# A third operand pair for the context tiles, low parts also on POOL, x's squares and scaling ahead of its columns, and eight context tiles in front of x's first columns

## The chip, the cores and the metric

The kernel runs on one core of a Trainium2 chip. The core has a matrix engine (TensorE, PE in the profile, with its weight loads as PEld), a vector engine (VectorE, DVE), an activation engine (ScalarE, ACT), a general engine (GpSimd, POOL) and a queue that issues most of the transfers (SyncE, SP). The metric is the device time of one execution in microseconds. Before the change it is 2383.04 us, the median of three runs from 2377.91 to 2387.13.

## The reference

One layer over 2048 latent tokens of width 1024, behind a prefix of 256 context tokens. All data is fp32.

```python
hc = modulate(rmsnorm(ctx, norm_mix), csh1, csc1)          # context, 256 tokens
logf_f, k_f, logf_b, k_b, vc = hgrn2_gates(hc @ w_in[:, :1536], ...)   # 4 heads x (forward gate, backward gate, value)
hf_c = advance_state(0, k_f, vc, cumsum(logf_f))           # final context state of each head, forward
hb_c = advance_state(0, flip(k_b), flip(vc), cumsum(flip(logf_b)))

h = modulate(rmsnorm(x, norm_mix), sh1, sc1)               # latent, 2048 tokens
p = h @ w_in                                               # 3584 columns: gates, value, query, output gate, two SGU halves
o = concat(bidirectional gated scan starting from hf_c, hb_c;  chunked spatial gating unit)
x = x + g1 * (o @ w_out)
x = x + g2 * conv_ffn(modulate(rmsnorm(x, norm_ffn), sh2, sc2), w_up, conv_w, conv_b, w_down)
return rmsnorm(x, norm_final)
```

`sh1, sc1` and `csh1, csc1` come from a small matrix product of `silu(c)` and `silu(c_ctx)` with `w_ada`. The change touches only the first part: the normalised context, its twelve projections (four heads, three each), the first 1024 latent tokens, and the order of their projections.

## The kernel before, in words

**Products of high and low parts.** Each fp32 operand is split into a rounded high part and a low part, the difference. ACT makes the high part with a copy, another engine subtracts it from the original (`split`, L137 and L138). A product then takes three matmuls: high x high, high x low, low x high. The tiles are called `whi`, `wlo` (weights), `chl` and `cll` (context), `xh` and `xl` (latent).

**Tiles and banks.** A tile of weights is 1024 x 128, so one tile has 1024 elements in each of 128 partitions, and 8 blocks along the contraction. A context tile multiplies it with the 256 context tokens: 24 matmuls of 256 columns. A bank of x multiplies it with 512 latent tokens: 24 matmuls of 512 columns, and two banks use one weight tile. `run_banks` (L523 and following) runs over a list of banks. At the start of each bank it splits the weights of the current and the next key where that hasn't been done, and loads raw weights one further ahead while context tiles are among the next three. Raw weights have three buffers, split weights have two pairs (`whi0`, `wlo0`, `whi1`, `wlo1`); `w_free` lists the free ones. A pair becomes free when the last bank of its key has been issued; the split that takes it then waits for the products that read it. A finished bank stays in one of three PSUM banks `pj` until ACT has read it (the sink).

**The order of the first banks.** `seq` gives it by letters: c a context tile (twelve of them: forward gate, backward gate, value of head 0, then head 1 and so on), g the output gate of latent head 0 (two banks: the first half of the 1024 tokens, then the second), v its value, q its query, s and t the SGU banks of heads 0 and 1 (Gelu on ACT, the others use sigmoids or copies). Then the gate banks of head 0 follow (`back`).

**The prologue** is written out by hand (`manual_schedule`): the order of the instructions on each engine is the order of the lines. It loads `w_ada` in four groups of 2 MB (`load_ada`, halves of 1 MB), squares and scales the context rows, transposes them, makes the modulation vectors (`ada_products`, `ada_rows`, `ada_columns`), and from them the context columns by `ctx_mod`, for k = 0 to 3 when the scale's first half is there and for k = 4 to 7 (`LAST`) after the second half. `keep_busy(n)` issues n products of the identity that nothing reads. In between it opens the first two context tiles with their blocks 0 to 3. Outside of the prologue the order on an engine is chosen when the program is built, by priorities and estimated durations; instructions passed through `pin` keep their order.

**x's columns.** Four row blocks of x (`xg`, 512 tokens) are squared on ACT with their sum (`x_square`), turned into a scale on POOL (`rstd`), scaled on DVE (`x_scale`), transposed on TensorE and modulated in `x_first`: `x_mod` has DVE compute the shifted value from PSUM, ACT the rounded high part, and DVE the low part. `x_start` does that for the first 512 tokens (`x0a`), then for the second (`x0b`, tiles `xk`). The first g bank waits for `x0a`, the second for `x0b`. `x_second` prepares the other 1024 tokens and stores them to DRAM; it must be through before the gate banks of head 0.

**Pumps.** Side work is written as generators in two queues (`bg_q`, `hg_q`). `slot()` is called after a bank and, in banks of 512 columns, between blocks; it advances a queue by one step when the estimated TensorE time `T.t` has passed the step's due time (the number it yielded). `need` forces all steps up to a mark.

Of the kernel before, what the change touches and what calls it, by code (L numbers as in the profile page):

```python
# [18 lines left out]
P = 128  # L19
# [69 lines left out]
def tile_trunk(ctx, tc, x, c, cx, c_ctx, w_ada, b_ada, norm_mix, norm_ffn, w_in, hg_norm, sgu_g, sgu_b,  # L89
# [105 lines left out]
    with es1:  # L195
# [16 lines left out]
        def keep_busy(n):  # L212

            t = bank("pj")
            for i in range(n):
                T.matmul(t[:, :P], ident, ident, start=True, stop=True)
# [3 lines left out]

        w_raw, w_free = {}, [0, 1]

        def load_raw(key):
            raw = raw_tile().rearrange("p (k c) -> p k c", c=P)
            ld(raw, w_in[:, key[0]:key[0] + P].rearrange("(k p) c -> p k c", p=P))
            w_raw[key] = raw

        def split_w(key, eng=V):
            if key not in w_raw:
                load_raw(key)  # L230
            raw, at = w_raw.pop(key), w_free.pop(0)
            hi = p1.tile([P, NK, P], F32R, tag=f"whi{at}", name="whi", align_bytes=AL)
            lo = p1.tile([P, NK, P], F32R, tag=f"wlo{at}", name="wlo", align_bytes=AL)
            split(hi, lo, raw, eng)
            return hi, lo, at
# [99 lines left out]
        with tc.manual_schedule():  # L335
# [9 lines left out]
            load_ada(1)  # L345
            load_ada(3, 0)
            load_raw((HW, CTX))
            load_ada(3, 1)
            S.activation(sg, cc, AF.Sigmoid)
# [34 lines left out]
            ctx_products(0, range(4))  # L384
            keep_busy(16)
            ada_products(3, 0, 4)
            nxt[HW, CTX] = split_w((HW, CTX))
            ada_products(3, 4, 8)
            ada_rows(3)
            opened[HW, CTX] = bank("pj")  # L390
            ctx_products(HW, range(2))
            ada_columns(3)
            ctx_products(HW, range(2, 4))
            ss0 = x_sums()
            for k in LAST:
                ctx_mod(k)
            x_square(xg[:1], ss0, keep=lambda i: i)
        xl = p1.tile([P, NK, TH], F32R, tag="xl", name="xl", align_bytes=AL)
        xh = p1.tile([P, NK, TH], F32R, tag="xh", name="xh", align_bytes=AL)

        def x_first(g0, xs):
            for k in range(NK):
                pt = bank("mi")
                for i in range(4):
                    pin(T.transpose(pt[:, i * P:(i + 1) * P], xs[i][:, k * P:(k + 1) * P], ident))
                sl = slice(g0 * P, g0 * P + 512)
                x_mod(pt, 0, k, xh[:, k, sl], xl[:, k, sl], 512, V)
                if k % 2:
                    yield 1.6
# [3 lines left out]
        def x_start():  # L413
            xk = [pk.tile([P, 2, D], F32, tag="K", name="xk", bufs=2, align_bytes=AL) for i in range(2)]
            xs = [xk[i // 2][:, i % 2, :] for i in range(4)]
            ss, ss2 = ss0, x_sums()
            for q in range(2):
                x_square(xg[2 * q + 1:2 * q + 3], ss, 2 * q + 1)
                for i in range(2 * q, 2 * q + 2):
                    pin(ld(xs[i], x_rows[4 + i]))  # L420
                if q:
                    x_scale(xg, ss)
                yield 2.0 + 3.0 * q
            for i, w in enumerate(x_first(0, xg)):
# [98 lines left out]
        def run_banks(banks, peek=None):  # L523
# [3 lines left out]
            for i, (col, n0, n, sink, pre) in enumerate(banks):  # L527
                if pre is not None:
                    pre()
                up = list(dict.fromkeys(keys[i:] + tail))  # L530
                for key in up[:2]:
                    if key not in nxt:
                        nxt[key] = split_w(key)
                if len(up) > 2 and up[2] not in w_raw and up[2] not in nxt and any(k[1] == CTX for k in up[:3]):
                    load_raw(up[2])
                hi, lo, at = nxt[keys[i]]
# [13 lines left out]
                if keys[i] not in keys[i + 1:]:  # L550
                    w_free.append(nxt.pop(keys[i])[2])

# [529 lines left out]
        seq = []  # L1082
        for item in "c c c c c c g c g v c v q c q s c s s c s t c t t t".split():
            seq.append(parts[item].pop(0))
# [795 lines left out]
```

## Time and profile before

| | |
|---|---|
| median of three runs | 2383.04 us (2377.91 to 2387.13) |
| the profiled execution | 2386.56 us, span 2384.8 us |
| TensorE busy | 2343.6 us, 98% |
| VectorE busy | 1597.3 us, 67% |
| ScalarE busy | 1041.6 us, 44% |
| GpSimd busy | 873.5 us, 37% |
| granted clock, mean | 0.996 |

The profile is one execution. Each row of a timeline is the start, the duration and the engine of an instruction or of several merged ones, its line in the kernel, the operation, the tiles out<-in, the shape, and in square brackets how long the engine was idle before it and what ended that. Rows of groups give the count, the busy time and the mean duration in ns. Rows of stretches give the busy time of every engine between two times. Matmuls overlap, so the distance between two starts says more than the duration of one.

### The profile page before, as it was taken

Reading aid. Unit: us, or ns where it says so; the run is one execution under the profiler, and the core shown is the slowest. Engines: PE = TensorE matmul, PEld = TensorE weight load, DVE = VectorE, ACT = ScalarE, POOL = GpSimd, SP = SyncE. Lnnn points to the kernel's source line nnn. Section 1 sums busy time; section 2 is a strip of 40 time slices with the busy share of each in tenths; the row PEclk is TensorE's granted clock in tenths of the full one; section 3 lists DMA queues with packets and bytes.
Section 4 is the critical chain, followed back from the end, with each engine's and each line's share of the span. In section 5 each row is a group of like instructions: output and inputs, shape, how many; then the busy total and the mean of one; then the engine's idle time right before and its main releaser. Section 6 shows DMA issues by size and latency. Waiting matters only on the chain.

```text
span 2384.8 us, 37077 instructions
## 1 busy us (share of the span) xinstructions
PE 2343.6 (98%) x14155; PEld 1933.1 (81%) x14155; DVE 1597.3 (67%) x2168; ACT 1041.6 (44%) x1814; POOL 873.5 (37%) x787
## 2 busy tenths in 40 slices
PE   7999999999999999999999999999999999999998
PEld 6887878778888877887788888888888888888887
DVE  3757795465687775665786666559777764776876
ACT  3654444443444543544544444344444443332343
POOL 0022111110122231003787877878788860000002
PEclk8999999999999999999999999999999999999999
DMA  8365444373445426679532222742322249734745
GB/s 310 115 198 182 160 152 163 135 239 107 155 160 186 151 90 221 210 229 298 181 99 93 75 91 85 277 152 84 104 79 94 86 137 386 258 127 159 222 150 203
DMA packets 304088, 393.59 MB, mean 165 GB/s; under 512 B 32646, under 2 KB 215710, under 8 KB 300838
## 3 DMA queue, kind: packets, MB, share of 16 engines
q1 hardware_dynamic: 300620, 390.46, 48.9%
q8 instruction: 111, 1.82, 0.3%
q10 hardware_dynamic: 3289, 0.76, 0.2%
q14 instruction: 68, 0.55, 0.1%
HBM read 283.60 MB, written 107.55 MB: 164 GB/s over the span
## 4 chain that ended last, share of the span: by engine, by line
PE 50%; issue 2%; POOL 1%; DMA 1%; DVE 0%; ACT 0%; SPq 0%; POOLq 0%; ACTq 0%; DVEq 0%
PE ux L70 19%; PE dn L70 16%; PE uz L70 14%; DMA raw<-in_w_up_dram 1%; POOL rr L1740 0%; DMA yf<-yd 0%; POOL Al L138 0%; DMA xn<-cv 0%; POOL ra L1739 0%; POOL ra L1737 0%; DVE fl L138 0%; PE ux L74 0%; ACT jk L1728 0%; ACT yst L137 0%; POOL raw L1254 0%
## 5 line engine op out<-in xcount | busy, mean ns | idle before, releaser
L1445 DVE SCALAR_TENSOR_TENSOR dn<-gp,taps,dn 128x1024 f32<-128x1024 f32 x352 | 448.2, 1285 | 97.1 <-ACT dn L1442 92.7
L70 PE MATMUL dn<-thl,mhl 128*128 128x512 f32 x1680 | 381.0, 389 | 0.0
L70 PEld LDWEIGHTS dn<-thl,mhl 128*128 128x128 f32 x1680 | 315.3, 188 | 65.6 <-issue 0.2
L138 POOL TENSOR_TENSOR Al<-raw,Ah 128x512 fp32r<-128x512 f32 x264 | 341.6, 1309 | 70.7 <-ACT Ah L137 40.3
L70 PE MATMUL pj<-xh,whi 128*128 128x512 f32 x896 | 366.8, 410 | 0.0
L70 PE MATMUL pj<-xl,whi 128*128 128x512 f32 x896 | 352.3, 393 | 0.0
L70 PE MATMUL pj<-xh,wlo 128*128 128x512 f32 x896 | 351.3, 392 | 0.0
L137 ACT CAST Ah<-raw 128x512 fp32r<-128x512 f32 x264 | 163.1, 620 | 242.5 <-PE ux L70 125.0
L70 PE MATMUL ux<-xah,Ah 128*128 128x512 f32 x528 | 205.9, 390 | 0.4 <-ACT keep L1509 0.3
L70 PEld LDWEIGHTS pj<-xh,whi 128*128 128x128 f32 x896 | 168.6, 188 | 39.0 <-issue 7.2
L70 PEld LDWEIGHTS pj<-xh,wlo 128*128 128x128 f32 x896 | 168.7, 188 | 35.9
L70 PEld LDWEIGHTS pj<-xl,whi 128*128 128x128 f32 x896 | 169.2, 189 | 29.8 <-DVE xl L257 0.6
L70 PE MATMUL dn<-wo,o 128*128 128x512 f32 x768 | 182.3, 394 | 0.0
L70 PE MATMUL uz<-yf,Ah 128*128 128x512 f32 x704 | 174.0, 389 | 0.0
L70 PEld LDWEIGHTS dn<-wo,o 128*128 128x128 f32 x768 | 142.1, 188 | 29.0
L589 POOL TENSOR_TENSOR K<-K,tot 128x512 f32<-128x512 f32 x40 | 61.2, 1530 | 259.4 <-DVE K L589 152.6
L70 PE MATMUL ux<-yf,Ah 128*128 128x512 f32 x528 | 155.4, 389 | 0.0
L70 PEld LDWEIGHTS uz<-yf,Ah 128*128 128x128 f32 x704 | 132.1, 188 | 27.4
L70 PE MATMUL ux<-xah,Al 128*128 128x512 f32 x528 | 141.8, 390 | 1.6 <-POOL Al L138 1.6
L70 PE MATMUL ux<-xal,Ah 128*128 128x512 f32 x352 | 137.1, 389 | 0.0
L1737 POOL TENSOR_SCALAR ra<-ss 128x1 f32<-128x1 f32 x8 | 3.2, 397 | 359.5 <-ACT jk L1728 359.5
L138 DVE TENSOR_TENSOR wlo<-raw,whi 128x1024 fp32r<-128x1024 f32 x68 | 83.6, 1230 | 74.8 <-ACT whi L137 63.7
(333 smaller groups left out, 4243.4 us busy)
## 6 DMA issues: line engine op xcount, KB each, us to landing
raw<-in_w_up_dram SPq DMA_DIRECT2D x88, 512.0 KB
mr<-m SPq DMA_DIRECT2D x85, 512.0 KB
raw<-in_w_in_dram SPq DMA_DIRECT2D x68, 512.0 KB
sT<-wd SPq DMA_DIRECT2D x88, 256.0 KB
raw<-in_w_ada_dram SPq DMA_DIRECT2D x32, 512.0 KB
yf<-yd SPq DMA_DIRECT2D x14, 1024.0 KB
m<-cv SPq DMA_DIRECT2D x22, 544.0 KB
raw<-in_w_down_dram SPq DMA_DIRECT2D x22, 512.0 KB
```

The lines of the kernel that those rows point to most:

```text
L70: return self.engine.matmul(out, lhsT, rhs, **kw)
L137: keep(S.copy(hi, raw))
L138: (eng or G).tensor_sub(lo, raw, hi.bitcast(F32))
L589: e.tensor_mul(view(K2, row * W + o, src), view(K, o, src), view(tot, t0, [[4, n], [ts, 2], [0, B]]))
L1445: V.scalar_tensor_tensor(out=cr, in0=gt[:, t // 3:t // 3 + RH, t % 3:t % 3 + GW], scalar=taps[:, t * NF + f:t * NF + f + 1], in1=cr, op0=A ...
L1737: G.tensor_scalar(out=a, in0=ss, scalar1=plus, scalar2=None, op0=ALU.add)
```

## The change

The third pair of operand tiles lies in the buffers of two tiles that are needed only later (`qs` and `T1`), and only context tiles may use it. `pair` chooses a pair: the third if it is free, or else the one that has been free longest. `run_banks` splits one key further ahead where the next free pair is the third, loads raw weights up to two keys ahead, and has every other split of a context tile subtract on GpSimd in place of VectorE. The third pair is given up when fewer than six context tiles are left. In the prologue the last half of `w_ada` is loaded ahead of the second context tile's weights; the filler products go from 16 to 20; the second context tile is no longer opened there and is split after the modulation vectors; the third context tile is split there, with its low part on GpSimd; and all four row blocks of x are squared there. `x_start` then starts with a pause and the scaling. For odd k the low part of x's columns in `x_first` is subtracted on GpSimd. In `seq` eight context tiles, not six, come before the first g bank, and all twelve come before the first q bank.

```diff
--- before.py
+++ after.py
@@ -218,19 +218,25 @@
         def raw_tile():
             return p1.tile([P, D], F32, tag="raw", name="raw", bufs=3)
 
-        w_raw, w_free = {}, [0, 1]
+        w_raw, w_free, w_more, n_split = {}, [2, 0, 1], [2], []
 
         def load_raw(key):
             raw = raw_tile().rearrange("p (k c) -> p k c", c=P)
             ld(raw, w_in[:, key[0]:key[0] + P].rearrange("(k p) c -> p k c", p=P))
             w_raw[key] = raw
 
+        def pair(key):
+            return max([a for a in w_free if a < 2 or key[1] == CTX], key=lambda a: (a == 2, -w_free.index(a)), default=None)
+
         def split_w(key, eng=V):
             if key not in w_raw:
                 load_raw(key)
-            raw, at = w_raw.pop(key), w_free.pop(0)
-            hi = p1.tile([P, NK, P], F32R, tag=f"whi{at}", name="whi", align_bytes=AL)
-            lo = p1.tile([P, NK, P], F32R, tag=f"wlo{at}", name="wlo", align_bytes=AL)
+            raw, at = w_raw.pop(key), pair(key)
+            w_free.remove(at)
+            pool, tags = (ph, ("qs", "T1")) if at == 2 else (p1, (f"whi{at}", f"wlo{at}"))
+            kw = {} if at == 2 else {"align_bytes": AL}
+            hi = pool.tile([P, NK, P], F32R, tag=tags[0], name="whi", **kw)
+            lo = pool.tile([P, NK, P], F32R, tag=tags[1], name="wlo", **kw)
             split(hi, lo, raw, eng)
             return hi, lo, at
 
@@ -343,9 +349,8 @@
             load_ada(0)
             load_raw((0, CTX))
             load_ada(1)
-            load_ada(3, 0)
+            load_ada(3)
             load_raw((HW, CTX))
-            load_ada(3, 1)
             S.activation(sg, cc, AF.Sigmoid)
             V.tensor_mul(cs2.rearrange("p k w -> p w k"), cc, sg)
             V.tensor_copy(cs4[:, :, :2], cs2)
@@ -382,19 +387,16 @@
             ada_columns(1)
             opened[0, CTX] = bank("pj")
             ctx_products(0, range(4))
-            keep_busy(16)
-            ada_products(3, 0, 4)
+            keep_busy(20)
+            ada_products(3, 0, 8)
+            ada_rows(3)
+            ada_columns(3)
             nxt[HW, CTX] = split_w((HW, CTX))
-            ada_products(3, 4, 8)
-            ada_rows(3)
-            opened[HW, CTX] = bank("pj")
-            ctx_products(HW, range(2))
-            ada_columns(3)
-            ctx_products(HW, range(2, 4))
-            ss0 = x_sums()
             for k in LAST:
                 ctx_mod(k)
-            x_square(xg[:1], ss0, keep=lambda i: i)
+            nxt[2 * HW, CTX] = split_w((2 * HW, CTX), G)
+            ss0 = x_sums()
+            x_square(xg, ss0, keep=lambda i: i)
         xl = p1.tile([P, NK, TH], F32R, tag="xl", name="xl", align_bytes=AL)
         xh = p1.tile([P, NK, TH], F32R, tag="xh", name="xh", align_bytes=AL)
 
@@ -404,7 +406,7 @@
                 for i in range(4):
                     pin(T.transpose(pt[:, i * P:(i + 1) * P], xs[i][:, k * P:(k + 1) * P], ident))
                 sl = slice(g0 * P, g0 * P + 512)
-                x_mod(pt, 0, k, xh[:, k, sl], xl[:, k, sl], 512, V)
+                x_mod(pt, 0, k, xh[:, k, sl], xl[:, k, sl], 512, G if k % 2 else V)
                 if k % 2:
                     yield 1.6
 
@@ -413,14 +415,14 @@
         def x_start():
             xk = [pk.tile([P, 2, D], F32, tag="K", name="xk", bufs=2, align_bytes=AL) for i in range(2)]
             xs = [xk[i // 2][:, i % 2, :] for i in range(4)]
-            ss, ss2 = ss0, x_sums()
-            for q in range(2):
-                x_square(xg[2 * q + 1:2 * q + 3], ss, 2 * q + 1)
-                for i in range(2 * q, 2 * q + 2):
-                    pin(ld(xs[i], x_rows[4 + i]))
-                if q:
-                    x_scale(xg, ss)
-                yield 2.0 + 3.0 * q
+            ss2 = x_sums()
+            yield 5.0
+            x_scale(xg, ss0)
+            for i in range(2):
+                pin(ld(xs[i], x_rows[4 + i]))
+            yield 5.0
+            for i in range(2, 4):
+                pin(ld(xs[i], x_rows[4 + i]))
             for i, w in enumerate(x_first(0, xg)):
                 if i in (1, 2):
                     x_square(xs[2 * i - 2:2 * i], ss2, 2 * i - 2)
@@ -528,11 +530,13 @@
                 if pre is not None:
                     pre()
                 up = list(dict.fromkeys(keys[i:] + tail))
-                for key in up[:2]:
-                    if key not in nxt:
-                        nxt[key] = split_w(key)
-                if len(up) > 2 and up[2] not in w_raw and up[2] not in nxt and any(k[1] == CTX for k in up[:3]):
-                    load_raw(up[2])
+                for j, key in enumerate(up[:3]):
+                    if key not in nxt and pair(key) in ((0, 1, 2) if j < 2 else (2,)):
+                        nxt[key] = split_w(key, G if key[1] == CTX and len(n_split) % 2 else V)
+                        n_split.append(key)
+                for key in up[2:3 + len(w_more)]:
+                    if key not in w_raw and key not in nxt and any(k[1] == CTX for k in up[:3]):
+                        load_raw(key)
                 hi, lo, at = nxt[keys[i]]
                 hiT, loT = (chl, cll) if n == CTX else (xh, xl)
                 pj = opened.pop(keys[i], None)
@@ -548,7 +552,13 @@
                 sink()(n0, n, pj[:, :n])
                 slot()
                 if keys[i] not in keys[i + 1:]:
-                    w_free.append(nxt.pop(keys[i])[2])
+                    at = nxt.pop(keys[i])[2]
+                    if at == 2 and len([k for k in keys[i:] if k[1] == CTX]) < 6:
+                        w_more.clear()
+                    elif at == 2:
+                        w_free.insert(0, at)
+                    else:
+                        w_free.append(at)
 
         def tile_banks(col, sink, W=TH, pre=None):
             return [(col, n0, min(512, W), sink, pre if n0 == 0 else None) for n0 in range(0, W, 512)]
@@ -1080,7 +1090,7 @@
               (front[1][0], 512, 512, front[1][3], lambda: need(bg_q, "x0b"))]
         parts = {"c": ctx_banks, "g": xa, "v": front[2:4], "q": front[4:6], "s": sgu_banks(0, 0), "t": sgu_banks(0, 1)}
         seq = []
-        for item in "c c c c c c g c g v c v q c q s c s s c s t c t t t".split():
+        for item in "c c c c c c c c g c c g v c v c q q s s s s t t t t".split():
             seq.append(parts[item].pop(0))
         assert not any(parts.values())
         seq += with_post(back, ctx_last)
```

## The prediction

> **What bounds the kernel now.** I read the page first, then busy time by stretch, then TensorE's timeline in the stretches where it is idle or slow.
>
> ```profile
> PE 2343.6 (98%) x14155; PEld 1933.1 (81%) x14155; DVE 1597.3 (67%) x2168; ACT 1041.6 (44%) x1814; POOL 873.5 (37%) x787
> PE 50%; issue 2%; POOL 1%; DMA 1%; DVE 0%; ACT 0%; SPq 0%; POOLq 0%; ACTq 0%; DVEq 0%
> ```
> ```profile
> 41.00:97.10 56.10, 49.63 (x298) 42.90 (x297) 45.98 (x73) 33.87 (x60) 2.42 (x4) 0.91 0.46 139
> 44.00:47.00 3.00, 3.00 (x16) 3.00 (x16) 1.28 (x3) 1.05 (x3) 0.00 (x0) 0.50 0.96 363
> 47.00:51.50 4.50, 1.74 (x9) 1.08 (x9) 1.50 (x2) 3.57 (x6) 1.22 (x2) 0.88 0.37 112
> 51.50:57.30 5.80, 5.80 (x28) 5.80 (x29) 4.01 (x6) 0.92 (x3) 0.00 (x0) 0.50 0.66 186
> 64.00:68.00 4.00, 3.96 (x27) 2.98 (x26) 4.00 (x8) 3.70 (x7) 0.00 (x0) 1.00 0.47 140
> 76.00:81.00 5.00, 2.87 (x21) 2.10 (x20) 5.00 (x8) 2.82 (x5) 0.00 (x0) 1.00 0.15 42
> 130.00:200.00 70.00, 68.88 (x382) 57.42 (x382) 47.55 (x110) 38.50 (x64) 24.08 (x31) 1.00 0.57 183
> ```
> Columns of the second fence: stretch, length, then busy time of PE, PEld, DVE, ACT, POOL, the granted clock, DMA share, GB/s. TensorE sets the end: 98% busy, and first in the chain. So the change is worth what it takes out of TensorE's losses, and those lie in one place. I number the context tiles c0 to c11.
>
> ```profile
> 41.92 0.39 PE L70 MATMUL pj<-ch,whi 128*128 128x256 f32 x1 [0.78 <-ACT whi L137]
> 43.18 0.38 PE L70 MATMUL pj<-ch,wlo 128*128 128x256 f32 x1 [0.76 <-DVE wlo L138]
> 50.02 0.38 PE L70 MATMUL pj<-ch,whi 128*128 128x256 f32 x1 [1.54 <-ACT whi L137]
> 58.02 0.28 PE L70 MATMUL pj<-ch,wlo 128*128 128x256 f32 x1
> 58.14 0.28 PE L70 MATMUL pj<-ch,whi 128*128 128x256 f32 x1
> 63.32 0.60 PE L74 MATMUL mi<-ident,cS 128*128 128x128 f32 x4
> 63.76 1.04 PE L74 MATMUL mi<-ident,xg 128*128 128x128 f32 x8
> 80.61 0.66 PE L74 MATMUL mi<-ident,xk 128*128 128x128 f32 x4 [1.47 <-ACT xh L256]
> 104.98 0.39 PE L70 MATMUL pj<-xh,wlo 128*128 128x512 f32 x1
> 105.21 0.39 PE L70 MATMUL pj<-xh,whi 128*128 128x512 f32 x1
> ```
> Matmuls overlap, so I count by their starts: a context product takes 0.12 us (58.02 to 58.14), an x product 0.23, a transpose 0.11; at clock 0.50 a context product takes 0.21 (28 instructions in the 5.80 us from 51.5). From 41.0 to 97.1 us TensorE did five context tiles (c2 to c6, 24 products each) and three x banks (24 each); the other 106 of its 298 instructions are transposes and small products. That is 120 x 0.119 + 72 x 0.228 + 106 x 0.11 = 42.4 us, in 56.1. **13.7 us are lost there**, in three ways: waits for the next tile's split operand (c2 at 41.9 and 43.2, c3 at 50.0); about nine microseconds at half clock right behind those waits, some 4 us of loss; and the wait for x's second group of columns around 76 to 81, while DVE is busy all the time. From 97 to 200 almost nothing is lost (68.88 of 70 busy at the end).
>
> **The change part by part.** The prologue first.
>
> ```profile
> 29.33 3.73 PE L70 MATMUL pj<-ident 128*128 128x128 f32 x32
> 32.99 1.96 PE L70 MATMUL pj<-wa,cs 128*32 128x128 f32 x64
> 30.07 1.05 ACT L137 CAST whi<-raw 128x1024 fp32r<-128x1024 f32 x1 [5.06 <-DMA raw<-in_w_in_dram]
> 36.01 0.17 DVE L304 TENSOR_TENSOR a<-sc,bc 128x8 f32<-128x8 f32 x1 [0.70 <-PE sc L74]
> 36.47 0.56 ACT L320 ACTIVATE ch<-mi,s,a 128x256 fp32r<-128x256 f32 x1 [5.35 <-DVE a L306]
> 39.92 0.43 DVE L322 TENSOR_TENSOR cl<-xfl,ch 128x256 fp32r<-128x256 f32 x1
> ```
> Four more fillers (8 of 32 instructions that took 3.73) push the last modulation products 0.9 us back, so the scale is ready near 37.1 rather than 36.4. The filler covers a load, the 1 MB half of the modulation weights, which is now issued ahead of c1's weights; c1's weights land later by that megabyte, 2.6 us at the 390 GB/s of the page, so near 32.7, still ahead of their new place behind the scale. There c1's low part (1.22) stands on DVE in front of the last four context columns: they end near 41.5, not 40.35 (the 0.7 later scale and the 1.22, less 0.7 in which DVE waits for ACT there today). Twelve of c1's products leave the gap before the scale and go after it, where they fill the wait for those columns. c0 and c1 are done at 42.0 against 41.1 (41.92 less the idle 0.78): **0.9 lost**.
>
> ```profile
> L243 ACT ACTIVATE xjk<-xg 128x1024 bf16<-128x1024 f32 x3 | 3.2, 1060 | 0.0
> L137 ACT CAST whi<-raw 128x1024 fp32r<-128x1024 f32 x7 | 7.3, 1047 | 5.2 <-PE pj L70 4.4 <-ACT xh L256 0.8
> L138 DVE TENSOR_TENSOR wlo<-raw,whi 128x1024 fp32r<-128x1024 f32 x7 | 8.5, 1219 | 6.2 <-ACT whi L137 6.0
> L613 DVE TENSOR_TENSOR_SCAN cS<-cS,ones_r 128x256 f32<-128x256 f32 x3 | 2.0, 682 | 0.0
> L254 DVE TENSOR_SCALAR xfl<-mi,a,s 128x512 f32<-128x512 f32 x10 | 7.6, 798 | 0.0
> L257 DVE TENSOR_TENSOR xl<-xfl,xh 128x512 fp32r<-128x512 f32 x10 | 6.5, 680 | 0.2 <-ACT xh L256 0.2
> L249 DVE TENSOR_SCALAR xg<-xg,rs 128x1024 f32<-128x1024 f32 x4 | 2.7, 748 | 0.0
> ```
> ```profile
> 41.78 0.38 ACT L558 ACTIVATE cS<-pj 128x256 f32<-128x256 f32 x1
> 73.88 1.36 DVE L257 TENSOR_TENSOR xl<-xfl,xh 128x512 fp32r<-128x512 f32 x2 [0.17 <-ACT xh L256]
> ```
> ```profile
> L138 POOL TENSOR_TENSOR Al<-raw,Ah 128x512 fp32r<-128x512 f32 x264 | 341.6, 1309 | 70.7 <-ACT Ah L137 40.3
> ```
> ```profile
> 139.00 0.75 POOL L257 TENSOR_TENSOR sp<-xfl,sp 128x256 fp32r<-128x256 f32 x1 [0.23 <-ACT sp L256]
> 141.82 1.32 POOL L257 TENSOR_TENSOR sp<-xfl,sp 128x256 fp32r<-128x256 f32 x1 [2.08 <-ACT sp L256]
> ```
> **Low parts on POOL.** No row has a 1024-element one. From below: 2 x 1.309 = 2.6 us. From above: the same 256-element subtraction took 0.75 and 1.32, so 2.6 x 1.76 = 4.6. I take 3.3, nearer the lower end, because DVE subtracts only part of the time. The Trainium skill, "GPSIMD Engine Reference", section 3.1, gives about 2.6 cycles per element at 1.2 GHz, an estimate of 2.2 us; by it c2 below would lose 0.5. Its section 1 says that POOL's SBUF interfaces are shared with VectorE; the 1.32 row agrees.
>
> **c2.** The third pair lets it be split ahead of c0's end. Its high part follows the last context column on ACT (39.5 to 40.5), its low part on POOL ends near 43.8. TensorE is free at 42.0 and has two products that don't need it: **1.6 lost** (0.9 to 2.9).
>
> **The four squares** stand on ACT behind that, 4 x 1.06 to 1.26, to about 45; what queues behind them are the four sigmoids of c0 and c1 (0.38 each, some 1.1 with their overlap; they free PSUM banks) and c3's high part. That is then ready at 47.0 and its low part (V) at 48.2, while c2 ends at 46.4: **1.6 lost** (0 to 2.5). c3 starts 3 us sooner than now.
>
> **The clock.** The trace shows half clock for 3.4 us from 43.7 and 6.8 from 50.6, behind stretches with waits. The waits of c2 and c3 are shorter, not gone; I count two such spells: **3.0 lost** (0 to 4.5). The Trainium skill, "TensorE: Matmul & The Clock Gate", Part 1, says that a window of about 3.4 us decides, and that it runs freely; the spells agree with its length, and by that rule the number of spells in the changed kernel also depends on where a wait falls. By the rule that only an idle window throttles, waits of 1.6 would cost nothing and the sum would be 3 better; the row of 44 to 47, behind two waits of 0.8 us, speaks against it.
>
> **c4 to c7.** From here a split uses a pair that was freed a tile earlier (third pair), so the copy needn't wait for the products before; the alternate low parts on POOL (1.05 + 3.3, against 2.9 us of a tile) start two tiles ahead. I allow **1.0** (0 to 3).
>
> **x's columns.** Squares done early, x_scale runs at about 48 to 51. DVE then has 8 x 0.80 + 4 x 0.68 for x's columns (the other four low parts go to POOL), two context low parts (2.4) and the scans of two context heads with their products (four of 0.68, four shorter ones I put at 0.42): 4.4. Done near 68. TensorE by then has 11.5 for c4 to c7, 3.5 for transposes and 3.4 for context states behind c3's end at 52.5 (48.2, its last 22 products, and one half-clock spell): near 71. The columns, finished today at 75.2 (row 73.88) with DVE full, no longer come last, with 3 us to spare. c8 and c9 after the first x bank cover the second group, today's wait at 76 to 81. But c9 is between the two banks of one key: one pair is held, the third retired after c7, so its split starts when c8 ends: 1.05 + 3.3, against transposes and the second x bank. I take **1.5** (0 to 4.4) for both.
>
> **Behind it.** The context tiles leave the SGU banks, so sigmoids and Gelus alternate less:
> ```profile
> L693 ACT ACT_TABLE_LOAD x2 | 2.6, 1283 | 0.0
> ```
> Each load is 1.28 us of ACT; TensorE's idle there is 1.1 us in 70, so I take 0.4 won (0 to 1.1). The second half of x, which begins behind x's second group, moves with it:
> ```profile
> 88.22 0.82 SPq L442 DMA_DIRECT2D xk<-in_x_dram x2
> 201.39 0.36 SPq L460 DMA_DIRECT2D xh_d<-sp  x1
> ```
> It takes 113 us today and frees the buffers of the first gate tiles. If it ended 8 us later, their sigmoids would wait; three PSUM banks (16 us of products) cover that, so nothing.
>
> **Sum.** Losses 0.9 + 1.6 + 1.6 + 3.0 + 1.0 + 1.5 = 9.6 in place of 13.7, and 0.4 won later: 4.5 us. The profiled execution took 2386.56 (span 2384.8 and 1.8 around it), so 2382.1; the median of the runs, 2383.04, lies 3.5 below it, so **2378.5**.
>
> **Rivals.** (A) Nearly all loss goes: no half clock, c3 and c9 covered by other products. Left are 0.9 and c2's 0.9: 12 us won, 2371. For it: DVE and ACT had room from 41 to 60. Against: the four squares in a block. (B) Slower: POOL's low parts gate TensorE. At 4.6 us, c2 loses 1.3 more, c4 1.7, c6 0.6, c9 4.2, and two more half-clock spells 3.0: 10.8, so 6.3 slower than before, 2389. It decides from about 4 us per low part, if a further clock spell comes with it. For it: the 1.32 row. Against: c4 to c8 can start early. (C) The wait only moves: x's columns, with POOL's subtractions at 2 us and context low parts ahead of them on DVE, end at 72 or later, TensorE waits 4 again before the first x bank: 2382.5. For it: DVE was full from 64 to 68 and from 76 to 81. Against: it sheds six low parts and eight subtractions, 12.8 us.
>
> **Chances.** Forecast 0.42, A 0.25, C 0.20, B 0.13. The runs of before spread over 9 us, so 0.5% (12 us) is about what can be told from no change. Faster by that needs under 2371: over half of A and a little of the forecast, 0.17. Slower needs over 2395: part of B, 0.05. The range takes in A and most of B: 2366 to 2390; the forecast alone is 2374 to 2383.
>
> **What would show it.** Right: c2 starts near 42 and c3 near 47; POOL's 1024-element rows at 3 to 3.6; squares in a block from 40.5 to 45; one or two half-clock spells before 60; first x bank ahead of 72, no gap at the second group; c9 waiting for its low part. Wrong: any low part above 4, a half-clock spell behind 60, new gaps from 97 to 200, or c3 later than 50.

## The result and the profile after

The changed kernel takes **2395.77 us** (median of 6 runs, 2393.42 to 2398.19) against 2383.35 of the kernel before beside it (6 runs, 2377.91 to 2387.13): 12.4 us more, ratio 1.0053, 95% interval 1.0038 to 1.0067. The forecast was 2378.5. The profiled execution took 2394.83 us with a span of 2393.0, so 8.3 more than the one of before, 2386.56. That one lay 3.2 above its median, so the two profiles show less than the medians do. The 4 us between the two differences are seen in no profile.

First a line of the page of the kernel after, then its windows, then one window of before for comparison. The line numbers of after are 6 to 13 higher than those of before. The columns of the windows are stretch, length, busy time and count of PE, PEld, DVE, ACT and POOL, the granted clock, DMA share and GB/s.

```profile
PE 2343.8 (98%) x14163; PEld 1936.2 (81%) x14163; DVE 1598.6 (67%) x2155; ACT 1035.8 (43%) x1810; POOL 895.4 (37%) x800
```
```profile
41.00:60.00 19.00, 15.04 (x117) 14.01 (x117) 14.44 (x15) 13.17 (x26) 8.92 (x5) 1.00 0.60 193
60.00:82.00 22.00, 18.69 (x128) 17.40 (x128) 20.14 (x33) 15.41 (x29) 5.25 (x4) 0.92 0.56 170
82.00:130.00 48.00, 43.92 (x267) 38.21 (x268) 26.89 (x36) 21.84 (x40) 12.89 (x11) 0.96 0.33 99
130.00:200.00 70.00, 69.62 (x351) 57.47 (x349) 38.80 (x98) 30.00 (x51) 22.32 (x28) 1.00 0.59 191
200.00:230.00 30.00, 26.87 (x126) 22.04 (x126) 18.39 (x28) 14.00 (x25) 5.54 (x8) 0.89 0.58 178
```
```profile
41.00:60.00 19.00, 14.70 (x80) 13.70 (x79) 11.22 (x18) 9.55 (x19) 1.22 (x2) 0.73 0.69 209
```

The stretch the change was made for did improve: 117 matmuls from 41 to 60 in place of 80, and the clock 1.00 in place of 0.73. Some 33 of the 117 are products of c0 and c1 that the kernel before had finished by 42; what was won shows at c5, whose first product starts at 59.37 in place of 60.38, although the prologue was late. **POOL's busy time there went from 1.2 to 8.9 us, and DVE, which was to be relieved, went up**: 14.4 us for 15 instructions, against 11.2 for 18. What was won is lost again behind 60.

The same instruction later in both kernels gives the sum (TensorE's timeline, before and then after):

```profile
708.41 1.47 PE L74 MATMUL mi<-ident,K 128*128 128x128 f32 x12
```
```profile
717.34 1.47 PE L74 MATMUL mi<-ident,K 128*128 128x128 f32 x12
```

It is 8.9 us later, so the whole difference of the two profiles, 8.2 us of span, arises in the front. The table counts TensorE's loss there as the prediction did: the distance from one matmul's start to the next, less 0.228, 0.119 or 0.11 us for its size. It is good to about 1 us. The kernels below the first two are the experiments of the next section. Each row is one execution: that of E5 is the fastest of its 12 (2378.98, their median 2385.38), so its row shows less than E5 usually loses.

| us lost | 40 to 60 | 60 to 80 | 80 to 100 | 100 to 180 | 180 to 220 |
|---|---|---|---|---|---|
| before | 9.9 | 3.3 | 0.4 | 1.7 | 0.4 |
| after | 7.9 | 2.0 | 8.1 | 0.2 | 6.5 |
| E1 weights' low parts on DVE | 4.2 | 5.1 | 2.8 | 0.5 | 4.3 |
| E2 all low parts on DVE | 4.2 | 1.7 | 2.1 | 1.1 | 6.3 |
| E3 old order of banks | 5.5 | 7.2 | 5.3 | 0.5 | 0.9 |
| E5 both (E2 and E3) | 4.0 | 6.8 | 0.8 | 1.5 | 0.8 |
| E12 before, fewer fillers | 5.8 | 4.2 | 0.6 | 0.9 | 0.4 |

To these come some 3.6 us by which the prologue is late. A gain of 3.3 from 40 to 80 and of 1.5 from 100 to 180 stands against 7.7 more from 80 to 100 and 6.1 more from 180 to 220: 12.6 in all. Near 410 us the same instruction is 10.3 later, near 708 it is 8.9. So a part is given back behind 220; the rest is the inaccuracy of the count.

**The prologue.** After:

```profile
27.03 1.94 PE L70 MATMUL pj<-wa,cs 128*32 128x128 f32 x32 [1.16 <-DMA wa<-in_w_ada_dram]
...
32.02 4.63 PE L70 MATMUL pj<-ident 128*128 128x128 f32 x40
36.57 1.96 PE L70 MATMUL pj<-wa,cs 128*32 128x128 f32 x64
```
```profile
39.77 0.56 ACT L326 ACTIVATE ch<-mi,s,a 128x256 fp32r<-128x256 f32 x1 [4.88 <-DVE a L312]
```

The same instruction in E4 below, which has the prologue of before:

```profile
38.71 0.56 ACT L326 ACTIVATE ch<-mi,s,a 128x256 fp32r<-128x256 f32 x1 [6.34 <-DVE a L312]
```

The first context column with the second half of the scale is made at 39.77, not at 36.47. The products ahead of it start 3.6 us later: the group of `w_ada` before it landed 1.2 later in this execution (its products began at 25.84 before), 0.9 is the eight filler instructions more, as foreseen, and most of the rest is a half-clock spell (the stretch from 27.8 to 32.0 was granted 0.53). But the 36.47 of before is itself early: with the same prologue it is 38.71 in E4, 38.32 in E6 and 38.67 in E7. So about 1 us of the lateness can be put down to the change, and some 2 to the two executions.

**DVE stands still while POOL subtracts.** Groups by line of POOL and of DVE, after, in the stretch from 40 to 110 (for POOL to 120). Columns: count, busy time, mean ns of one, idle time before.

```profile
L138 POOL TENSOR_TENSOR wlo<-raw,whi 128x1024 fp32r<-128x1024 f32 x5 | 12.4, 2488 | 33.1 <-ACT whi L137 33.1
L263 POOL TENSOR_TENSOR xl<-xfl,xh 128x512 fp32r<-128x512 f32 x8 | 11.0, 1374 | 29.5 <-ACT xh L262 29.5
```
```profile
L260 DVE TENSOR_SCALAR xfl<-mi,a,s 128x512 f32<-128x512 f32 x16 | 12.4, 804 | 5.3 <-PE mi L74 2.9 <-POOL xl L263 2.2
...
L263 DVE TENSOR_TENSOR xl<-xfl,xh 128x512 fp32r<-128x512 f32 x8 | 7.9, 987 | 0.1
L623 DVE TENSOR_TENSOR_SCAN cS<-cS,ones_r 128x256 f32<-128x256 f32 x4 | 4.9, 1236 | 1.0 <-ACT cS L568 1.0
L255 DVE TENSOR_SCALAR xg<-xg,rs 128x1024 f32<-128x1024 f32 x4 | 4.9, 1278 | 1.3 <-POOL rs L132 1.3
L471 DVE CAST msk<-mf 32x128 uint8<-32x128 f32 x8 | 3.7, 466 | 0.1
L328 DVE TENSOR_TENSOR cl<-xfl,ch 128x256 fp32r<-128x256 f32 x4 | 3.7, 948 | 0.1
```

The same groups in E2, where nothing but the engine of the subtractions differs:

```profile
L263 DVE TENSOR_TENSOR xl<-xfl,xh 128x512 fp32r<-128x512 f32 x16 | 10.7, 684 | 0.3
L623 DVE TENSOR_TENSOR_SCAN cS<-cS,ones_r 128x256 f32<-128x256 f32 x4 | 2.7, 686 | 0.1
L255 DVE TENSOR_SCALAR xg<-xg,rs 128x1024 f32<-128x1024 f32 x4 | 2.7, 750 | 1.3 <-DMA xk<-in_x_dram 1.3
...
L471 DVE CAST msk<-mf 32x128 uint8<-32x128 f32 x8 | 1.7, 217 | 0.1
L328 DVE TENSOR_TENSOR cl<-xfl,ch 128x256 fp32r<-128x256 f32 x4 | 1.6, 424 | 0.1
```

POOL took five low parts of weights (1.22 each on DVE) and eight of x (0.684 each) from DVE, 11.6 us. But the five other groups grew: 8 x 0.30 + 4 x 0.55 + 4 x 0.53 + 8 x 0.25 + 4 x 0.52 = **10.8 us. Of 11.6 us taken off DVE, 10.8 came back as standing time**, and at moments that POOL chose. In the timeline of the three engines (after; start, duration, engine, idle before it) it looks like this:

```profile
43.34 2.37 POOL L138 TENSOR_TENSOR wlo<-raw,whi 128x1024 fp32r<-128x1024 f32 x1 [27.42 <-ACT whi L137]
...
57.24 2.67 POOL L138 TENSOR_TENSOR wlo<-raw,whi 128x1024 fp32r<-128x1024 f32 x1 [1.45 <-ACT whi L137]
...
95.29 2.35 POOL L138 TENSOR_TENSOR wlo<-raw,whi 128x1024 fp32r<-128x1024 f32 x1 [0.42 <-ACT whi L137]
```
```profile
43.47 2.52 DVE L328 TENSOR_TENSOR cl<-xfl,ch 128x256 fp32r<-128x256 f32 x1
...
52.80 4.87 DVE L255 TENSOR_SCALAR xg<-xg,rs 128x1024 f32<-128x1024 f32 x4 [1.29 <-POOL rs L132]
...
57.59 2.88 DVE L623 TENSOR_TENSOR_SCAN cS<-cS,ones_r 128x256 f32<-128x256 f32 x1
...
95.74 0.69 DVE L1023 SCALAR_TENSOR_TENSOR sgt<-pj,sig 128x512 f32<-128x512 f32 x1
96.54 0.81 DVE L260 TENSOR_SCALAR xfl<-mi,a,s 128x512 f32<-128x512 f32 x1
```
```profile
46.04 0.39 PE L70 MATMUL pj<-cl,whi 128*128 128x256 f32 x1 [1.59 <-DVE cl L328]
...
50.30 0.39 PE L70 MATMUL pj<-ch,whi 128*128 128x256 f32 x1 [0.52 <-ACT whi L137]
...
51.56 0.39 PE L70 MATMUL pj<-ch,wlo 128*128 128x256 f32 x1 [0.76 <-DVE wlo L138]
...
62.19 0.39 PE L70 MATMUL pj<-ch,wlo 128*128 128x256 f32 x1 [2.33 <-DVE wlo L138]
```

The last context column's subtraction, 0.42 us of work, begins 0.13 behind POOL and ends at 45.99, 0.28 behind POOL's end at 45.71; TensorE waits for it. The scan at 57.59, 0.69 of work, ends 0.56 behind POOL; c5's low part stands behind it on DVE, TensorE waits 2.33, and half clock follows to 65.8. But the two DVE instructions at 95.74 and 96.54, which read PSUM (`pj`, `mi`), run through POOL's subtraction at their normal length. The Trainium skill, "GPSIMD Engine Reference", section 1, says that the SBUF interfaces are shared and that there is contention with DVE instructions in a 2-port mode or with two SBUF inputs. The trace agrees as far as it goes: the groups that grew read only SBUF, and those with an input from PSUM did not. Whether the scaling and the cast, which have one SBUF input, run in such a mode it doesn't show.

**The second half of x.** In E2 and after, the new order loses again near 200 (after; SP's queue, DVE, TensorE, and one window):

```profile
101.28 1.41 SPq L444 DMA_DIRECT2D xk<-in_x_dram  x2
...
194.00 0.88 SPq L444 DMA_DIRECT2D xk<-in_x_dram  x1
```
```profile
202.51 1.42 DVE L255 TENSOR_SCALAR xk<-xk,rs 128x1024 f32<-128x1024 f32 x2 [6.33 <-POOL rs L132]
```
```profile
203.32 0.48 PE L74 MATMUL mi<-ident,xk 128*128 128x128 f32 x1 [3.13 <-DVE xk L255]
```
```profile
203.00:209.00 6.00, 5.68 (x20) 4.90 (x21) 4.21 (x8) 1.69 (x3) 1.15 (x2) 0.50 0.06 22
```

The first load is issued 13 us later than before (88.22), and the last at 194.0, in place of 175.91. The new order makes about half of the 13: without POOL's subtractions the first load is at 93.07 with it (E2) and at 86.18 with the old one (E5). The rows of the last load are squared and scaled by 203, while their transposes already stand at the head of TensorE's queue, because the gate banks of head 0 need them. TensorE waits 3.1 and then runs at half clock for 6 us.

### The profile page after: what moved, and what is told of

It reads as the page before. It is cut to its first block, busy times and chain, and to the rows that moved or that the text cites. A ratio compares the mean times of both kernels' runs of the same rounds, so it can differ in the third digit from the quotient of the medians.

```text
span 2393.0 us, 37095 instructions
## 1 busy us (share of the span) xinstructions
PE 2343.8 (98%) x14163; PEld 1936.2 (81%) x14163; DVE 1598.6 (67%) x2155; ACT 1035.8 (43%) x1810; POOL 895.4 (37%) x800
## 4 chain that ended last, share of the span: by engine, by line
PE 50%; issue 2%; POOL 1%; DVE 1%; ACT 0%; DMA 0%; SPq 0%; POOLq 0%; ACTq 0%; DVEq 0%
PE ux L70 20%; PE dn L70 15%; PE uz L70 15%; POOL rr L1750 0%; DVE dn L1455 0%; DMA xn<-cv 0%; POOL Al L138 0%; POOL ra L1749 0%; POOL ra L1747 0%; ACT jk L1738 0%; SPq L1545 0%; PE dn L74 0%; POOL raw L1264 0%; DVE odd L85 0%; DMA gs<-gp 0%
## 5 line engine op out<-in xcount | busy, mean ns | idle before, releaser
L138 DVE TENSOR_TENSOR wlo<-raw,whi 128x1024 fp32r<-128x1024 f32 x63 | 77.9, 1236 | 82.1 <-ACT whi L137 79.8
```

What stands on the lines that cost most here:

```text
L138: (eng or G).tensor_sub(lo, raw, hi.bitcast(F32))
```

## The experiments

The theory after the result had two parts. **Lock**: POOL's subtractions stop DVE. **Order**: twelve context tiles ahead of everything make `x_second` late. Rivals were that DVE is simply overloaded, so that giving it the subtractions back would make things worse; that the late prologue is the cause; and that the third pair or the closer loads of raw weights cost something themselves. All ratios are to the kernel before, run beside it on the same chip, with 95% intervals.

**E1: only the weights' low parts back to DVE** (x's stay on POOL)

```diff
-            nxt[2 * HW, CTX] = split_w((2 * HW, CTX), G)
+            nxt[2 * HW, CTX] = split_w((2 * HW, CTX))
...
-                        nxt[key] = split_w(key, G if key[1] == CTX and len(n_split) % 2 else V)
+                        nxt[key] = split_w(key)
```


> The changed kernel with every context weight's low part on VectorE; x's odd low parts stay on GpSimd. Theory lock (a VectorE instruction that meets a running GpSimd subtraction stands until it ends, 2.1 to 2.2 us each at 43.5, 52.8 and 57.6 in the trace after): these three stretched rows return to 0.43, 2.7 and 0.7 us, TensorE's waits at 44 and 59 shrink from 1.75 and 2.5 to under 1, and the kernel is 4 to 6 us faster than the changed one: 2390 to 2392. Rival load (VectorE has no room, so 6 x 1.22 us more on it cost as much as the lock): no difference from the changed kernel, 2395 to 2397.


2389.84 us, 1.0025 (1.0015 to 1.0035). By the ratios 0.28% of 2384, 6.7 us, of the 12.4 us come back, although DVE has five more subtractions to do.

**E2: x's low parts back to DVE too**

```diff
-                x_mod(pt, 0, k, xh[:, k, sl], xl[:, k, sl], 512, G if k % 2 else V)
+                x_mod(pt, 0, k, xh[:, k, sl], xl[:, k, sl], 512, V)
```


> As the first, and x's odd low parts on VectorE too, so that GpSimd subtracts nothing of the front. Theory lock: the stretched rows from 72 to 82 (1.90, 1.91 and 1.76 us) return to 0.9 and 0.7; eight subtractions of 0.68 come back on VectorE; about even with the first, 2389 to 2393. Rival load: VectorE is full from 60 to 90 again, 3 to 5 us slower than the first.


2386.64 us, 1.0015 (1.0005 to 1.0025): another 0.1%. The rival that DVE is overloaded falls. Both runs also take away the waits for a low part that is merely slower on POOL; here the trace has to separate the two. After, TensorE was idle for 2.2 us in two waits for a low part of POOL (0.95 and 1.24), and for 3.9 in two waits for DVE instructions that had stood or stood behind one (1.59 and 2.33). So lock holds for the larger part. What is left is the gap of `x_second`, in TensorE's waits from 27 to 230 (total, count, longest):

```profile
PE mi L74 <- DVE xk L255: 5.1, 2, 4.4
```

**E3: the old order of the banks, the rest as changed**

```diff
-        for item in "c c c c c c c c g c c g v c v c q q s s s s t t t t".split():
+        for item in "c c c c c c g c g v c v q c q s c s s c s t c t t t".split():
```


> The changed kernel with the order of the first banks as before the change (six context tiles, then g c g v c v q c q s c s s c s t c t t t). Theory order: the second half of x starts near 90 rather than 101 us and is through before the gate banks, so the gap of 3.3 us at 200 and the half clock behind it (5.8 us lost together) go, and the 1.9 us for the tile between the two g banks: 6 to 9 us faster than the changed kernel, 2387 to 2390. Rival front (all of the loss is made by the prologue and by GpSimd): 2394 to 2397.


2391.22 us, 1.0025 (1.0015 to 1.0035). The gap near 200 is gone (0.9 in the table), but the kernel gains less than foreseen: from 60 to 100 it loses 12.5 us. With fewer context tiles to cover x's columns, their lateness counts; E5, the same order without POOL's subtractions, loses 7.6 there.

**E4: the prologue and the start of x of before, the rest as changed**

```diff
-            keep_busy(20)
-            ada_products(3, 0, 8)
+            keep_busy(16)
+            ada_products(3, 0, 4)
...
-            x_square(xg, ss0, keep=lambda i: i)
+            x_square(xg[:1], ss0, keep=lambda i: i)
...
```


> The changed kernel with the prologue and the start of x's columns as before the change (16 fillers, second context tile opened early, one square in the prologue, third tile not split there). Theory: the second half of the modulation is ready at 36.4 to 37.6 rather than 39.7, the first two tiles are done near 41 rather than 46, but the third tile is split later; 2 to 4 us faster than the changed kernel, 2392 to 2394. Rival (the early squares are what makes x's columns ready): x's first columns come later and it is as slow as the changed kernel or slower, 2396 to 2400.


2394.38 us, 1.0041 (1.0027 to 1.0054). By the ratios 0.12%, 2.9 us, come back, but its interval overlaps that of the whole change. So this part of the change has at most a small net price; the run undoes the early squares as well, and a gain of one can hide a price of the other. A gap of 3 us for `x_second` remains.

**E5: E2 and E3 together**. What is left of the change is the third pair, the early squares and the prologue.

> The changed kernel with nothing subtracted on GpSimd in the front and with the old order of the first banks; left of the change are the third pair, the early squares and the prologue. Theory (two separate losses, the lock of some 9 us and the order of some 6): both gains add up, 2386.6 less 5 is 2381 to 2383, a little faster than the kernel before. Rival (the two share a cause, x's second group being late): no better than the better of the two, 2386 to 2388.


2385.38 us, 1.0003 (0.9991 to 1.0014). The loss is gone within the interval, so **the two edits together account for it**. What the order costs by itself is less sure: the intervals of E2 and E5 overlap, and 0.12%, 2.9 us, lies between them. But the gain expected of the rest isn't there. From 40 to 60 it loses 4.0 us in place of 9.9, from 60 to 80 6.8 in place of 3.3: with the context tiles done sooner, TensorE reaches x's second group sooner, and DVE, busy almost without a break from 52 to 80, finishes it no sooner.

**E6: before, with every other context low part on POOL and nothing else**

```diff
-                        nxt[key] = split_w(key)
+                        nxt[key] = split_w(key, G if key[1] == CTX and len(n_split) % 2 else V)
+                        n_split.append(key)
...
```


> The kernel before with one part of the change alone: every other context low part is subtracted on GpSimd, two pairs. Theory lock: five low parts of 2.4 to 2.65 us each in the place of 1.22, each on the way to TensorE (with two pairs a split starts when the tile before the last ends), and VectorE instructions stretched by up to 2.2 each: 4 to 9 us slower than before, 2389 to 2394. Rival (GpSimd is only another free engine): 0 to 2 us faster than before.


2391.79 us, 1.0033 (1.002 to 1.0045): one edit of the change, put alone into the old kernel, costs 0.33%, 7.9 us. On DVE a small cast that meets a low part is stopped in the same way (0.22 in E2). x's columns stand behind it, and TensorE waits 2.94 for them, up to 70.83. The other of the two waits in the first line (2.00, up to 86.53) meets no subtraction of POOL. TensorE also waits once for a low part of POOL itself (second line); before, its only wait for `xh` in this stretch was 1.5 us.

```profile
67.03 2.21 DVE L469 CAST msk<-mf 32x128 uint8<-32x128 f32 x1
```
```profile
PE mi L74 <- ACT xh L256: 4.9, 2, 2.9
PE pj L70 <- POOL wlo L138: 1.9, 1, 1.9
```

**E7: before with the third pair and raw loads two ahead only**

```diff
-        w_raw, w_free = {}, [0, 1]
+        w_raw, w_free, w_more, n_split = {}, [2, 0, 1], [2], []
...
-                for key in up[:2]:
-                    if key not in nxt:
-                        nxt[key] = split_w(key)
+                for j, key in enumerate(up[:3]):
+                    if key not in nxt and pair(key) in ((0, 1, 2) if j < 2 else (2,)):
+                        nxt[key] = split_w(key)
...
```


> The kernel before with the third pair alone (and raw weights two ahead): old prologue, old order, all low parts on VectorE. Theory: the waits of c3 at 47 to 51 and part of the half clock go, 2 to 5 us faster than before, 2380 to 2383. Rival (the wait at c3 stands on ScalarE behind squares and sigmoids, not on the pair): no difference, within 1 us of before.


2384.29 us, 1.0003 (0.999 to 1.0016): nothing either way, as the rival said. The pair lets the high part be made sooner (TensorE waits 0.8 for it, before 2.3), and the wait moves to the low part (before 1.5):

```profile
PE pj L70 <- DVE wlo L138: 3.9, 2, 3.1
```

**E8: E2 with `x_second` paced closer**

```diff
                 x_scale(xs, ss)
-                yield 6.0
+                yield 4.0
...
-                    yield 2.2
+                    yield 1.6
```


> The changed kernel with nothing subtracted on GpSimd in the front, new order kept, and the second half of x paced closer (after the scaling 4.0 in place of 6.0, between blocks 1.6 in place of 2.2), some 17 us earlier in all. Theory late (the new order loses at 190 to 210 only because the second half of x isn't through when the gate banks start): the gap of 4.6 us there goes, 5 to 7 us faster than the same kernel with the old pace (2386.6), 2380 to 2382. Rival (the order itself crowds that stretch): the gap stays or moves ahead into the SGU banks, 2385 to 2388.


2386.68 us, 1.0011 (1.0001 to 1.0021), as E2 and as the rival said. The one long wait for `xk` becomes seven short ones, and behind 180 TensorE waits for other tiles (all of the second line, 1.4 of the third):

```profile
PE mi L74 <- DVE xk L255: 3.9, 7, 1.1
PE mi L74 <- ACT sp L262: 2.5, 2, 1.6
PE mi L70 <- ACT ckt L633: 1.8, 3, 1.4
```

From 180 to 220 it loses 4.8 in place of 6.3, from 100 to 180 4.3 in place of 1.1. Yet the last load went at 172.50, ahead of the 175.91 of before, where nothing is lost. So the late `x_second` makes the gap in E2 and after, but an earlier one doesn't remove what the new order costs; what else the order crowds is not shown.

**E9, E10, E11: two ways to use what E5 has left.** E9 is E5 with 8 filler products in place of 20 (two instructions each). E10 is E5 with every other row block of the first 1024 tokens scaled on ACT. E11 is both.

```diff
-            keep_busy(20)
+            keep_busy(8)
```
```diff
+                if act and i % 2:
+                    keep(S.activation(xt, xt, AF.Copy, scale=r[:, i:i + 1]))
+                else:
+                    keep(V.tensor_scalar(out=xt, in0=xt, scalar1=r[:, i:i + 1], scalar2=None, op0=ALU.mult))
```


> This is the kernel with all low parts on VectorE and the old order of the banks (about 2385.4, ratio 1.0003), with 8 filler products in place of 20. Theory: the fillers stand ahead of the last modulation products, so the second half of the modulation is ready as soon as its weights have landed; where the load lands by about 32, 12 fewer fillers of 0.116 us bring everything behind forward by 1.0 to 1.4 us: 2383.5 to 2384.5. Rival: the load decides (its products began anywhere from 33.0 to 36.9 us in the profiles so far) and TensorE, left idle for longer, falls to half clock: 2385 to 2389, with a half-clock spell between 29 and 36 in the trace.


2380.4 us, 0.9991 (0.9979 to 1.0003): by the ratios 0.12% or 2.9 us better than E5, though the intervals overlap. The expectation counted one instruction of 0.116 us per filler; there are two, so 24 fewer, 2.8 us.

> The same kernel (about 2385.4) with every other row block of x's first 1024 tokens scaled on ScalarE in place of VectorE (four instructions of about 0.7 us leave VectorE, four of about 1.05 come to ScalarE). Theory: VectorE, full from 52 to 80 us there, holds x's columns back, and the waits ahead of the second group of columns (73 to 77) shrink by 2 to 3 us: 2382 to 2383.5, below the kernel before. Rival: ScalarE, which has 19 of 28 us in the same stretch and makes the high parts of the weights and of x's columns, becomes late instead, or the wait moves to the next split: 2385 to 2388.


2385.31 us, 1.0011 (1.0001 to 1.0022): no gain, as the rival said. The loss from 60 to 80 goes from 6.8 to 4.4, that from 40 to 60 from 4.0 to 6.0.

> Both of these edits together. If each gains for its own reason, the gains add: 2381 to 2382.5, 0.1% below the kernel before. If a wait only moves to the next operand that is late, it is as the kernel before within 2 us (2383 to 2387).


2377.35 us, 0.9984 (0.9972 to 0.9996): below the kernel before by 0.16%. Its interval overlaps that of E9, so the fillers may be the whole of it. It lies clear of E10's, from which only the fillers differ: 0.27%, 6.4 us.

**E12: before, with fewer fillers and nothing of the change**

```diff
-            keep_busy(16)
+            keep_busy(4)
```


> The kernel before with nothing of the change, but with 4 filler products in place of 16 ahead of the last modulation products. Theory: fillers that stand ahead of those products cost time in either kernel, so the 12 fewer gain here what they gained on the kernel with low parts on VectorE and the old order (there 2380.4 against 2385.4 us, ratio 0.9991 against 1.0003): 2379 to 2382, ratio 0.998 to 0.9995. Rival: here the wait for c2's split operand follows anyway, whose high part ScalarE makes behind the context columns and whose raw weights are loaded later, so the gain is lost in it: 2382.5 to 2385, ratio 0.9995 to 1.001.


2378.85 us, 0.9984 (0.9973 to 0.9996), 4.2 us below before's 2383.01. One edit of a number gives what E11 gives with all that is left of the change. The timeline and the window show part of why:

```profile
29.84 1.77 PE L70 MATMUL pj<-ident 128*128 128x128 f32 x8
31.54 2.13 PE L70 MATMUL pj<-wa,cs 128*32 128x128 f32 x64
```
```profile
41.00:60.00 19.00, 15.48 (x113) 14.70 (x112) 14.31 (x23) 11.61 (x22) 1.22 (x2) 0.91 0.83 252
```

In no profile do the modulation products wait for their load behind the fillers. They start at 31.54 here, at 32.99 before, at 36.57 after and at 30.25 in E11: their load has landed by then, and the fillers delay them. Against before that is 1.5 us sooner, although the eight that are left ran at half clock in this execution (0.22 each, 0.117 before). From 41 to 60 it was granted 0.91 in place of 0.73. Taken by the length of the fillers, 24 x 0.117, the gain is 2.8 of the 4.2 us; where the rest comes from is not settled by these profiles, since E4, E6 and E7, with 16 fillers, start the same products only at 34.85 to 35.24.

## Why the prediction was wrong

The sign was wrong, and 2395.77 lies above the range (2366 to 2390). By its own steps:

- **Low parts on POOL, the step that failed.** The prediction took 3.3 us for one (2.6 to 4.6). It measured 2.35 to 2.67, around the lower end; the 2.2 that the prediction has beside it was nearer. In the 1.32 row of before POOL, started at 141.82, was held up by DVE subtractions that ran from 141.00 to 142.55, and the prediction took that for the whole price of sharing: a longer time on POOL. The runs show the other side: DVE waits for POOL, up to a whole subtraction. The prediction counted 12.8 us taken off DVE and no price there. The price had to be put on DVE's queue, on every instruction reading only SBUF that meets one: 10.8 us of standing against 11.6 taken off. E1, E2 and E6 show it.
- **c2.** 1.6 foreseen for its low part. A wait of 1.59 came, but the equal number is chance, for it stood ahead of c2: POOL worked on c2's low part while the last context column stood on DVE. c2 itself had none; it was done near 49.7, foreseen 46.4, and 2.7 of that is the later scale.
- **The squares in a block, and c3.** ACT met c0's sigmoid between the first and the second square and waited 2.28 us for that stuck product. The scaling ran from 52.8 to 57.7, foreseen 48 to 51. c3's high part was used at 50.30, before at 50.0, not 3 us sooner; its two waits (0.52 and 0.76 idle, 1.6 between the starts) are the foreseen size.
- **The prologue.** Foreseen: scale ready near 37.1 and 0.9 lost. The first column behind it was 3.3 later than in the profile of before, and 1.1 later than in E4. The fillers' 0.9 was right; the landing and the half clock belong to this execution (with as many fillers, the same products began at 33.06 in E5). "The filler covers a load" is wrong: E9 and E12 took twelve of them away and gained about 3 and 4 us. The 390 GB/s that the prediction reads off the page stands in no row; its highest slice is 386. Nothing hangs on it.
- **The clock.** 3.0 for two spells before 60 were foreseen. From 41 to 60 there was none, the best part of the change and better than foreseen. They came later: at 62.4 to 65.8, once between 80 and 90, and at 203 to 209.
- **c4 to c7.** 1.0 foreseen, about 3.6 measured: 1.1 at 55.84 for a low part on POOL, and 2.5 at 62.19 for c5's behind the stopped scan.
- **x's columns and c9.** 1.5 foreseen. c9 waited for its low part on POOL as foreseen, 1.24. The second group, which c8 and c9 were to cover, did not come in time, and half clock followed: 8.1 us from 80 to 100. Waits after, TensorE's timeline:

```profile
82.59 1.16 PE L70 MATMUL mi<-cb,ckt 128*128 128x128 f32 x8 [1.56 <-ACT ckt L633]
...
85.18 0.30 PE L74 MATMUL mi<-ident,xk 128*128 128x128 f32 x1 [1.43 <-DVE xk L255]
...
97.70 0.39 PE L70 MATMUL pj<-ch,wlo 128*128 128x256 f32 x1 [1.24 <-POOL wlo L138]
```

- **`x_second`, the second step that failed.** Priced at nothing, because three PSUM banks cover it. They would cover a late sigmoid. What is late in after and E2 is the transposes, which are TensorE's own instructions, ahead of the products that should cover them. It costs 6.1 us more from 180 to 220; E3 and E5, with the old order, take it away; E8, with an earlier `x_second`, doesn't.
- **The rivals.** (B), POOL's low parts gate TensorE, 2389, named the right edit, and its mechanism made the smaller part: at about 2.5 us per low part, below the 4 from which it was to decide, TensorE waited 2.2 us for them in all. The larger part came through DVE and through the order, which no rival had. (C), the wait only moves, is what E5 and E7 show for the rest of the change.

Of the signs of being wrong, two came: half clock behind 60 and c3 later than 50. The new gap lies at 200 to 203, just behind the stretch named. Of the signs of being right, only c9's wait came; the first x bank began at 76.64, not ahead of 72.

## What to carry to other kernels

An elementwise step given to POOL isn't free for DVE because POOL is idle: ask which DVE instructions read only SBUF while it runs, and price the longest of them as if it stood behind POOL's instruction in one queue. Work that TensorE itself does for a later stage (transposes) can't be covered by TensorE's products once it stands ahead of them, so its due time has to be read against the new order of the banks. Products issued to bridge a load are pure delay where the load has already landed; look whether the next product has an idle time in front of it before adding more.

## What the hardware showed

- **DVE instructions that read only SBUF and POOL's subtractions stop each other, up to a whole instruction.** A 0.42 us subtraction took 2.52 beside POOL, a scan of 0.69 took 2.88, four scalings of 2.7 together took 4.87. It goes the other way too: a POOL subtraction of 1.29 took 1.84 where DVE's had begun 0.11 earlier. Mostly the one that starts first goes through, but not always: in E6 a DVE scan begun at 66.34, behind POOL's subtraction at 66.04, ran its normal 0.68, and POOL's took 3.13. DVE instructions with an input in PSUM were not stopped (0.69 and 0.81 inside POOL's 2.35).
- **Half clock followed some waits shorter than itself, but not all of them.** A wait of 2.33 us at 62 was followed by 3.4 us of half clock, one of 1.59 at 46 by none. Whether it depends on when a wait falls, these runs don't show.
- **The prologue's loads vary.** The same group of weights was used at 25.25 in E11 and at 27.03 after, and executions of one kernel spread over some 11 us (E12: 2375.88 to 2386.68), so single profiles of two kernels can differ by several microseconds for that reason alone.
